# A two-block trunk on one core: the second block's bias table is written to memory one row per query and read back with a shifted step; constant products stand at the first block's norms

## The chip, the core and the metric

The kernel runs on one core of one Trainium2 chip. The metric is the device time of one execution in microseconds (us). TensorE (PE) multiplies, VectorE (DVE) and ScalarE (ACT) work element by element, GpSimd (POOL) does some element work and issues accumulating DMAs, and SyncE (SP) issues all other DMAs. All DMAs of the core run on the same 16 DMA engines.

## The reference

Two blocks run one after the other on x of 512 tokens by 1024 channels, each with two layers. Every layer has projections, attention and a feed-forward part with norms in between. What the change touches is the bias of the second block's windowed attention: `rel` is key minus query, a bucket function maps it to one of 32 buckets, and 16 heads have one value for each bucket.

```python
rel = jnp.arange(KEY_SPAN)[None, :] - WINDOW - jnp.arange(ATTN_BLOCK)[:, None]
band_bias = rel_bias.astype(f32)[t5_bucket(rel)].transpose(2, 0, 1)
...
s = jnp.einsum("bqgrd,bkgd->bgrqk", qb, kb,
               preferred_element_type=jnp.float32) * scale + bias
```

For one head this is a 128 x 384 tile (query by key) whose every row is the row above moved right by one. The first block's norms, at which the table is made, are

```python
x = x + rms_norm(mixed @ w_out, attn_post_gain)
h = rms_norm(x, ffn_pre_gain)
x = x + rms_norm(conv_ffn(h, ffn_w_up, ffn_conv_w, ffn_conv_b, ffn_w_down), ffn_post_gain)
```

## The kernel before

**Weights.** All weights stream through the core in chunks of eight 128 x 128 tiles (class `Stream`). A chunk is loaded into `raw` by SP (512 KB, line 301), ACT writes its negative to `lo` (line 311), POOL issues a DMA that reads the chunk from memory a second time and adds it to `lo` (line 312, 512 KB), and ACT or POOL rounds `raw` to `h` (line 316 or 314). So `h + lo` is the weight in two parts; the page calls them wh and wl. Each tile takes three products (lines 489 to 491), 24 for a chunk. There are four buffers of each kind. When the program reaches chunk c it emits the load of chunk c+6 and the conversion of chunk c+3; what it emits on SP, POOL and ACT then stands in their queues in that order.

**The norms.** `post_norm` (line 1329) ends the attention part and the feed-forward part of each of the first block's two layers: four norms. It sums squares on PE (`stat`), reduces them on DVE, takes the root on ACT and the reciprocal on DVE, spreads the result over all partitions on PE (`statb`), and then, for eight channel tiles m, DVE forms y (line 1341), DVE or POOL adds it to x (line 1342), ACT makes h of the tile before (line 403) and DVE its remainder hl (line 404). Then the residual is stored (xf or xa, eight DMAs of 256 KB) and the next group of products starts on h. `keep_warm(n)` multiplies a matrix of ones n times and nobody reads the result. I call the norms 1 to 4 in order of time; the chunk whose first product follows a norm is c.

**The table.** `bias_table` is a generator that is stepped by the caller (`side.step`). Its second step forms one row of 512 values for each head (`btab`, 16 partitions) and stores it as `tab_d`. Then it takes one head per step: SP reads 128 overlapping rows, each one element on from the last (`brev`), a product with the exchange matrix `exch` reverses their order (`bex`), ACT copies the result (`bout`) and SP stores it in `bias_d`. Two such steps come before norm 1, and every norm takes four more: one ahead of `rstd_a`, one behind it, two behind `spread`.

**Its readers.** In the second block `load_bias(h)` (line 1787) reads one head's 128 x 384 tile, two heads ahead of its use at line 1937, 16 times in each layer.

All engines run their instructions in the order in which the program emits them. The functions that the change touches:

Of the kernel before, what the change touches and what calls it, by code (L numbers as in the profile page):

```python
# [10 lines left out]
F32 = mybir.dt.float32  # L11
F32R = mybir.dt.float32r
I32 = mybir.dt.int32
AF = mybir.ActivationFunctionType
# [3 lines left out]
T = 512  # L18
# [6 lines left out]
NB, NO = 2, 2  # L25
XD = 30
GA, GB, GC = 1, 4, 1
NWU, NKW = 13, 6
NEG = -1.0e30
BIG = 3.0e38  # L30
TINY = 1e-30
# [121 lines left out]
def _consts():  # L153
    parts = []
    pos = 0

    def add(name, a):
        nonlocal pos
        a = np.asarray(a, np.float32)
        _CS[name] = (pos, a.shape[1])  # L160
        parts.append(a)
        pos += a.shape[1]

    p = np.arange(128)
    r, c = p[:, None], p[None, :]
    add("ident", np.eye(128))
    add("exch", np.eye(128)[::-1])
    add("maskA", np.concatenate([np.where(c > r, 0, NEG), np.where(c <= r, 0, NEG)], 1))
    add("maskC", np.concatenate([np.zeros((128, 384)), np.where(c <= r, 0, NEG)], 1))
    add("le", r <= c)  # L170
    add("ge", r >= c)
    add("gt", r > c)
    add("lt", r < c)
    n = np.arange(32)
    ok = np.stack([((n * 16 + 31)[None, :] <= (128 * i + p)[:, None]) & (n < 31)[None, :] for i in range(4)], 1)
    add("c01", ok.reshape(128, 128))
    add("cneg", np.where(ok, 0, NEG).reshape(128, 128))
    add("invf", (10000.0 ** (-(p % 32) / 32.0))[:, None])
    add("sign", np.where(p % 64 < 32, -1.0, 1.0)[:, None])
    return np.concatenate(parts, 1)  # L180


CONST = _consts()
NCST = CONST.shape[1]

# [61 lines left out]
def trunk_kernel(ctx: ExitStack, tc: tile.TileContext, xT, positions, wts, cst_d, oh_d, rb_d, cw1_d,  # L247
                 prm1_d, prm2_d, outT):
    nc = tc.nc
    layers = 2  # L250
    ctx.enter_context(tc.manual_schedule())
    V, A, G, PE = nc.vector, nc.scalar, nc.gpsimd, nc.tensor
# [4 lines left out]
    dpool = ctx.enter_context(tc.tile_pool(name="dpool", bufs=1, space=bass.MemoryType.DRAM))  # L257
# [4 lines left out]
    def big(name, dt=F32):  # L262
        return pools["t"].tile([128, T], dt, tag="t", name=name)

    def small(n, name, bufs=2):
        return pools["s"].tile([128, n], F32, tag=name, name=name, bufs=bufs)
# [4 lines left out]
    def bank(name, hold=False):  # L271
        b = banks.pop(0)
        t = psum.tile([128, T], F32, tag=f"b{b}", name=name)
        if hold:
            held[id(t)] = (b, t)
        else:
            banks.append(b)
        return t

    def free(t):  # L280
        banks.append(held.pop(id(t))[0])
# [105 lines left out]
    def C(name):  # L387
        o, n = _CS[name]
        return cst[:, o:o + n]
# [48 lines left out]
    def rstd_a(sq, n, act=False):  # L438

        sq.sums(len(sq.p))  # L440
        ps = sq.stat
        v = small(4, "var")
        V.tensor_reduce(v, ps[:, 0:128 * len(sq.p)].rearrange("p (a j) -> p j a", j=128)[:, 0:4, :], AX.X, OP.add)
        free(ps)
        r4 = small(4, "rs")
        if act:
            A.activation(v, v, AF.Sqrt, bias=epst, scale=1.0 / n)
            V.reciprocal(r4, v)
            return r4
        t4 = small(4, "rt")  # L450
        V.tensor_scalar(v, v, 1.0 / n, EPS, op0=OP.mult, op1=OP.add)
        V.tensor_scalar(r4.bitcast(I32), v.bitcast(I32), -0.5, float(0x5F3759DF), op0=OP.mult, op1=OP.add)
        for _ in range(3):
            V.tensor_mul(t4, r4, r4)
            V.scalar_tensor_tensor(t4, t4, -0.5, v, op0=OP.mult, op1=OP.mult)
            V.scalar_tensor_tensor(r4, t4, 1.5, r4, op0=OP.add, op1=OP.mult)
        return r4
# [5 lines left out]
    def keep_warm(n):  # L463

        t = bank("warm")
        for _ in range(n):
            PE.matmul(t[:, 0:128], ones, ones, start=True, stop=True)

    def spread(r4):

        pb = bank("statb", True)
        for j in range(4):
            PE.transpose(pb[:, 128 * j:128 * j + 128], r4[:, j:j + 1].to_broadcast([128, 128]), ident)
        return pb
# [79 lines left out]
    def prep(x, gcol, late=False):  # L554

        hs, sq = [], Squares(late=late)

        def f(m):
            h, lo = big("h", F32R), big("hl", F32R)
            split(h, lo, x[m], scale=gcol[:, m:m + 1])  # L560
            hs.append((h, lo))
        return hs, sq, f
# [221 lines left out]
    def layer1(l, x, hs, sq, gnext, side):  # L784
# [419 lines left out]
        for m in range(KT):  # L1204
# [7 lines left out]
            run(g)  # L1212
        ms.clear()
        hs, sq3 = post_norm(x, ys, pc("g2"), sq2, pc("g3"), side)


# [69 lines left out]
        ffn_order(pair, down)  # L1286
        x = xn
        hs, sq = post_norm(x, ys, pc("g4"), sq4, gnext(), side)
        if l:
            side.finish()  # L1290
# [38 lines left out]

    def post_norm(x, ys, gcol, sq, gnext, side):  # L1330

        side.step(1)
        r4 = rstd_a(sq, D, act=True)
        side.step(1)
        R = spread(r4)
        side.step(2)
        keep_warm(NKW)
        hs, sqn, f = prep(x, gnext)
        for m in range(KT):
            y = ys[m]  # L1340
            V.scalar_tensor_tensor(y, y, gcol[:, m:m + 1], R, op0=OP.mult, op1=OP.mult)
            (V if m % 2 == 0 else G).tensor_add(x[m], x[m], y)
            if m:
                f(m - 1)
        f(KT - 1)
        free(R)
        return hs, sqn


    bias_d = dpool.tile([128, 16, 384], F32, name="bias_d")  # L1350

    def bias_table():

        oh = big("oh")
        nc.sync.dma_start(oh[0:33, :], oh_d)
        rb = small(16, "rb", bufs=2)
        nc.sync.dma_start(rb[0:32, :], rb_d)
        V.memset(rb[32:33, :], NEG)
        yield
        ps = bank("btab")  # L1360
        PE.matmul(ps[0:16, :], rb[0:33, :], oh[0:33, :], start=True, stop=True)
        tb_ = big("btab")
        V.tensor_copy(tb_[0:16, :], ps[0:16, :])
        tab_d = dpool.tile([16, T], F32, name="tab_d")
        nc.sync.dma_start(tab_d, tb_[0:16, :])
        rev = {}
        for h in range(18):
            if h < 16:
                rev[h] = big("brev")
                nc.sync.dma_start(rev[h][:, 0:384], bass.AP(  # L1370
                    tensor=tab_d.tensor, offset=tab_d.offset + h * T, ap=[[1, 128], [1, 384]]))
            if h >= 2:
                pb = bank("bex")
                PE.matmul(pb[:, 0:384], C("exch"), rev.pop(h - 2)[:, 0:384], start=True, stop=True)
                o = big("bout")
                A.activation(o[:, 0:384], pb[:, 0:384], AF.Copy)
                nc.sync.dma_start(bias_d[:, h - 2, :], o[:, 0:384])
            yield

    masks = []  # L1380
# [7 lines left out]
    def layer2(l, x, hs, sq, gnext):  # L1388
# [396 lines left out]
        bias = {}  # L1785

        def load_bias(h):
            if h < 16:
                bias[h] = big("bias")
                nc.sync.dma_start(bias[h][:, 0:384], bias_d[:, h, :])  # L1790

        bias["load"] = load_bias
        load_bias(0)
        load_bias(1)
        pieces = [p for h in range(2, 16) for p in at(4 * h - 8, 2, head(h))]
        pieces += rest + at(7, 1, kx)
        pieces += [p for g in (2, 3) for p in at(17 + 8 * (g - 2), 2, pieces_of(stack_k(K, g, lambda: kT[1]), 4))]
        units = []
        for a in range(8):
            nm, den = small(8, "nm", bufs=8), small(8, "den", bufs=8)  # L1800
            o = {}
# [18 lines left out]
            for e in range(2):  # L1820
                h = 2 * a + e
# [96 lines left out]
        for m in range(KT):  # L1918
            o = big("out")
# [30 lines left out]
    with tc.tile_pool(name="spool1", bufs=2) as pools["s"]:  # L1950
        x = []
        hs, sq, f = prep(x, col(1, 0, P1, "g1")())
        keep_warm(NWU)
        for m in range(KT):
            load_x(x, m)
            if m % 2:
                W.load((m + 3) // 2)
            if m == 5:
                nc.sync.dma_start(cst, cst_d)
        for m in range(KT):  # L1960
            if m % 2 == 0:
                W.conv(m // 2 + 1)
            f(m)
        load_params(1, 1)
        side = Fill(bias_table())
        x, hs, sq = layer1(0, x, hs, sq, col(1, 1, P1, "g1"), side)
        load_params(2, 0)
        x, hs, sq = layer1(1, x, hs, sq, col(2, 0, P2, "n1"), side)
# [43 lines left out]
```

## Time and profile before

| | |
|---|---|
| time, median of 3 runs | 3266.52 us (3254.92 to 3266.82) |
| profiled execution: time, span | 3263.05 us, 3261.3 us |
| PE busy | 3097.5 us, 95% of the span |
| ACT, DVE, POOL busy | 1885.1, 1752.6, 759.9 us (58, 54, 23%) |
| mean granted TensorE clock | 0.979 of full |
| DMA moved | 547.30 MB, 168 GB/s on average |

A busy share says that an instruction was under way; matmuls are pipelined, so PE's 95% is not 95% of its peak. The span runs from the first to the last instruction; the time has 1.75 us more around it.

### The profile page before, as it was taken

The numbers are of one execution on the slowest core, as the hardware profiler recorded it, in microseconds if no ns is written. First come the engines' busy times: TensorE is split into PE (matmuls) and PEld (weight loads), VectorE is DVE, ScalarE is ACT, GpSimd is POOL, SyncE is SP. The second block draws the span as 40 slices with busy tenths as digits, with TensorE's granted clock in tenths as the row PEclk, the third lists the DMA queues.
The fourth block names the chain that finished last, engine by engine and source line by source line (L and its number), as shares of the span: only waits on it lengthen the run. The fifth ranks groups of instructions, "written<-read, shape, count | busy, mean of one in ns | idle before, by whom it ended". The sixth has DMA issues, their size and how long they took to land. (4 is left out here: it accounts for less than half of the span.)

```text
span 3261.3 us, 40685 instructions
## 1 busy us (share of the span) xinstructions
PE 3097.5 (95%) x14604; PEld 2543.5 (78%) x14604; DVE 1752.6 (54%) x3431; ACT 1885.1 (58%) x3288; POOL 759.9 (23%) x770
## 2 busy tenths in 40 slices
PE   8999999999899999999998889999999888999998
PEld 7878878887778877888786668788888666888887
DVE  5577355153477635424378987341326898734132
ACT  4578556464357756645476567554556656755453
POOL 2222211111222221111135422111112542211110
PEclk8999999999899999999999999999999989999999
DMA  9744769887964487989774334789897534488975
GB/s 273 169 104 91 196 177 206 195 202 188 231 145 106 91 210 186 204 188 224 182 172 110 96 93 111 196 201 219 199 224 167 116 77 114 99 202 202 224 183 140
DMA packets 170277, 547.30 MB, mean 168 GB/s; under 512 B 20011, under 2 KB 29227, under 8 KB 170076
## 3 DMA queue, kind: packets, MB, share of 16 engines
q0 software_dynamic: 66240, 241.20, 43.5%
q1 hardware_dynamic: 103836, 303.50, 26.7%
q8 instruction: 116, 1.90, 0.3%
q14 instruction: 85, 0.70, 0.1%
HBM read 516.81 MB, written 19.96 MB: 165 GB/s over the span
## 5 line engine op out<-in xcount | busy, mean ns | idle before, releaser
L490 PE MATMUL acc<-h,wl 128*128 128x512 f32 x2464 | 971.7, 394 | 36.3 <-DMA wl<-in_wts 36.2
L489 PE MATMUL acc<-h,wh 128*128 128x512 f32 x2464 | 994.7, 404 | 0.8 <-ACT h L403 0.8
L491 PE MATMUL acc<-hl,wh 128*128 128x512 f32 x2464 | 969.5, 393 | 0.2
L312 POOL DMA_DIRECT2D wl<-in_wts x460 | 398.6, 866 | 2030.0 <-ACT wl L311 1837.0
L311 ACT ACTIVATE wl<-wraw 128x1024 fp32r<-128x1024 f32 x460 | 482.9, 1050 | 299.2 <-PE acc L490 271.9
L490 PEld LDWEIGHTS acc<-h,wl 128*128 128x128 f32 x2464 | 469.3, 190 | 134.3 <-DMA wl<-in_wts 42.8
L491 PEld LDWEIGHTS acc<-hl,wh 128*128 128x128 f32 x2464 | 468.0, 190 | 100.7 <-DVE hl L404 1.5
L489 PEld LDWEIGHTS acc<-h,wh 128*128 128x128 f32 x2464 | 469.4, 190 | 95.7 <-issue 5.3
L316 ACT ACTIVATE wh<-wraw 128x1024 fp32r<-128x1024 f32 x400 | 417.3, 1043 | 0.0
L489 PE MATMUL acc<-ah,wh 128*128 128x512 f32 x704 | 274.4, 390 | 0.0
L491 PE MATMUL acc<-al,wh 128*128 128x512 f32 x704 | 274.1, 389 | 0.0
L490 PE MATMUL acc<-ah,wl 128*128 128x512 f32 x704 | 274.0, 389 | 0.0
L674 PE MATMUL pt<-cst,p 128*128 128x128 f32 x752 | 144.0, 279 | 24.3 <-ACT p L1939 9.5
L1229 ACT ACTIVATE c<-u,prm 128x512 f32<-128x512 f32 x88 | 71.1, 815 | 145.1 <-DVE u L1225 145.1
L489 PEld LDWEIGHTS acc<-ah,wh 128*128 128x128 f32 x704 | 132.2, 188 | 27.4
L491 PEld LDWEIGHTS acc<-al,wh 128*128 128x128 f32 x704 | 132.2, 188 | 27.4
L490 PEld LDWEIGHTS acc<-ah,wl 128*128 128x128 f32 x704 | 132.2, 188 | 27.2
L1225 DVE TENSOR_TENSOR u<-acc,R 128x512 f32<-128x512 f32 x88 | 60.0, 687 | 173.3 <-PE acc L491 173.2
L1085 ACT ACTIVATE p<-p,nm 128x128 f32<-128x128 f32 x192 | 102.1, 532 | 62.6 <-DVE nm L1083 60.6
L680 ACT ACTIVATE pth<-pt 128x256 fp32r<-128x256 f32 (+2 forms) x320 | 130.7, 411 | 9.6 <-PE pt L674 7.1
L674 PEld LDWEIGHTS pt<-cst,p 128*128 128x128 f32 x752 | 93.3, 141 | 51.5 <-ACT p L1939 17.9
L1895 DVE TENSOR_TENSOR x<-x,acc 128x512 f32<-128x512 f32 x32 | 22.0, 688 | 185.3 <-PE acc L491 171.7
(334 smaller groups left out, 5103.0 us busy)
## 6 DMA issues: line engine op xcount, KB each, us to landing
wraw<-in_wts SPq DMA_DIRECT2D x460, 512.0 KB, 6.7
wl<-in_wts POOLq DMA_DIRECT2D x460, 512.0 KB, 7.1
bias<-bias_d SPq DMA_DIRECT2D x32, 192.0 KB, 2.6
x<-in_xT SPq DMA_DIRECT2D x16, 256.0 KB, 8.4
cw<-in_cw SPq DMA_DIRECT2D x16, 256.0 KB, 6.3
xf<-x SPq DMA_DIRECT2D x16, 256.0 KB, 2.1
x<-xf SPq DMA_DIRECT2D x16, 256.0 KB, 10.1
xs<-x SPq DMA_DIRECT2D x16, 256.0 KB, 5.8
```

The lines of the kernel that those rows point to most:

```text
L311: A.activation(lo, r, AF.Copy, scale=-1.0)
L312: G.dma_start(out=lo, in_=wts[c], accum_op=OP.add)
L316: A.activation(h, r, AF.Copy)
L489: PE.matmul(acc, wh, xh, start=first, stop=False)
L490: PE.matmul(acc, wl, xh, start=False, stop=False)
L491: PE.matmul(acc, wh, xl, start=False, stop=last)
L674: PE.transpose(pt[:, 128 * n:128 * n + 128], t[:, 128 * (kb - b0):128 * (kb - b0) + 128], ident)
L680: A.activation(th[:, 0:w], pt[:, 0:w], AF.Copy)
L1085: A.activation(p[:, 0:w], p[:, 0:w], AF.Exp, bias=nm[:, col:col + 1], scale=-1.0, accum_out=den[:, col:col + 1])
L1225: V.tensor_mul(u, acc, st3["R"])
L1229: A.activation(c, u, AF.Identity, bias=cb[:, idx:idx + 1], scale=cw[:, 88 + idx:89 + idx])
L1895: V.tensor_add(x[m], x[m], acc)
```

## The change

`bias_table` keeps its row of 512 values per head but no longer stores `tab_d`, reads it back reversed, multiplies or copies. For each head one DMA reads the head's row, which lies in one partition of `btab`, 128 times and writes 128 rows of 512 values to `bias_d`, which is now 16 x 128 x 512 (256 KB a head). `load_bias` reads row q from element 127-q on, by a step of 511 between rows. `exch` leaves the constants. In `post_norm` all four steps come first, `keep_warm(3)` stands ahead of `spread`, and the products behind it are nine where they were six.

```diff
-NWU, NKW = 13, 6
+NWU, NKW = 13, 9
...
-    add("exch", np.eye(128)[::-1])
...
-        side.step(1)
+        side.step(4)
         r4 = rstd_a(sq, D, act=True)
-        side.step(1)
+        keep_warm(3)
         R = spread(r4)
-        side.step(2)
         keep_warm(NKW)
...
-    bias_d = dpool.tile([128, 16, 384], F32, name="bias_d")
+    bias_d = dpool.tile([16, 128, T], F32, name="bias_d")
...
-        tab_d = dpool.tile([16, T], F32, name="tab_d")
-        nc.sync.dma_start(tab_d, tb_[0:16, :])
-        rev = {}
-        for h in range(18):
-            if h < 16:
-                rev[h] = big("brev")
-                nc.sync.dma_start(rev[h][:, 0:384], bass.AP(
-                    tensor=tab_d.tensor, offset=tab_d.offset + h * T, ap=[[1, 128], [1, 384]]))
-            if h >= 2:
-                pb = bank("bex")
-                PE.matmul(pb[:, 0:384], C("exch"), rev.pop(h - 2)[:, 0:384], start=True, stop=True)
-                o = big("bout")
-                A.activation(o[:, 0:384], pb[:, 0:384], AF.Copy)
-                nc.sync.dma_start(bias_d[:, h - 2, :], o[:, 0:384])
+        for h in range(16):
+            nc.sync.dma_start(bias_d[h], tb_[h:h + 1, None, :].to_broadcast([1, 128, T]))
             yield
...
-                nc.sync.dma_start(bias[h][:, 0:384], bias_d[:, h, :])
+                nc.sync.dma_start(bias[h][:, 0:384], bass.AP(
+                    tensor=bias_d.tensor, offset=bias_d.offset + h * 128 * T + 127, ap=[[T - 1, 128], [1, 384]]))
```

On ACT at norm 1 stood, before, from the last squares of the norm to the next weights:

```order
L417 ACTIVATE sq<-acc 128x512
L1200 ACTIVATE y<-acc 128x512
L1376 ACTIVATE bout<-bex 128x384
L447 ACTIVATE var<-var,epst 128x4
L1376 ACTIVATE bout<-bex 128x384 x3
L403 ACTIVATE h<-x,prm 128x512 x8
L311 ACTIVATE wl<-wraw 128x1024
```

and now (the line numbers of the changed file are one lower there):

```order
L416 ACTIVATE sq<-acc 128x512
L1199 ACTIVATE y<-acc 128x512
L446 ACTIVATE var<-var,epst 128x4
L402 ACTIVATE h<-x,prm 128x512 x8
L310 ACTIVATE wl<-wraw 128x1024
```

The four copies are gone from between the root (`var`) and the first h. On PE at the same norm stood, before:

```order
L491 MATMUL acc<-ml,wh 128x512
L1374 MATMUL bex<-brev,cst 128x384
L434 MATMUL stat<-ones,sq 128x1 x4
L1374 MATMUL bex<-brev,cst 128x384
L473 MATMUL statb<-cst,rs 128x128 x4
L1374 MATMUL bex<-brev,cst 128x384 x2
L467 MATMUL warm<-ones 128x128 x6
L489 MATMUL acc<-h,wh 128x512
```

and now:

```order
L490 MATMUL acc<-ml,wh 128x512
L433 MATMUL stat<-ones,sq 128x1 x4
L466 MATMUL warm<-ones 128x128 x3
L472 MATMUL statb<-cst,rs 128x128 x4
L466 MATMUL warm<-ones 128x128 x9
L488 MATMUL acc<-h,wh 128x512
```

Products that waited for a DMA were exchanged for products that wait for nothing. SP's queue from the weights ahead of the table's row (`btab`) held, before, up to the second head's store:

```order
L301 DMA wraw<-in_wts 128x1024 x2
L1365 DMA tab_d<-btab 16x512
L1370 DMA brev<-tab_d 128x384
L301 DMA wraw<-in_wts 128x1024
L1370 DMA brev<-tab_d 128x384
L301 DMA wraw<-in_wts 128x1024 x4
L1370 DMA brev<-tab_d 128x384
L1377 DMA bias_d<-bout 128x384
L1370 DMA brev<-tab_d 128x384
L1377 DMA bias_d<-bout 128x384
```

and now up to the weights behind the stores:

```order
L300 DMA wraw<-in_wts 128x1024 x2
L1363 DMA bias_d<-btab 128x1x512
L300 DMA wraw<-in_wts 128x1024
L1363 DMA bias_d<-btab 128x1x512
L300 DMA wraw<-in_wts 128x1024 x4
L1363 DMA bias_d<-btab 128x1x512 x4
L372 DMA xf_4259<-x 128x512 x8
L300 DMA wraw<-in_wts 128x1024 x55
```

Two writes stand ahead of the last five weight loads before norm 1, four stand together ahead of the stores, and the weights of the feed-forward part come behind all of them. At norms 2 and 3 four writes stand so, at norm 4 two.

## Rows read from the trace of the kernel before

**Rows 1.** Page, costliest groups: busy us, mean ns, idle before and its releaser.

```profile
L490 PE MATMUL acc<-h,wl 128*128 128x512 f32 x2464 | 971.7, 394 | 36.3 <-DMA wl<-in_wts 36.2
```

**Rows 2.** Timeline of norm 1: start us, us, engine, line, operation, idle before.

```profile
414.04 0.65 PE L473 MATMUL statb<-cst,rs 128*128 128x128 f32 x4
415.50 0.69 DVE L1342 TENSOR_TENSOR x<-x,y 128x512 f32<-128x512 f32 x1
416.11 0.74 DVE L1341 SCALAR_TENSOR_TENSOR y<-y,prm,statb 128x512 f32<-128x512 f32 x1
416.83 0.91 PE L1374 MATMUL bex<-brev,cst 128*128 128x384 f32 x2 [1.50 <-DMA brev<-tab_d]
...
417.78 0.49 ACT L1376 ACTIVATE bout<-bex 128x384 f32<-128x384 f32 x1 [1.92 <-PE bex L1374]
418.17 1.32 ACT L403 ACTIVATE h<-x,prm 128x512 fp32r<-128x512 f32 x2
...
418.91 0.75 DVE L404 SCALAR_TENSOR_TENSOR hl<-x,prm,h 128x512 fp32r<-128x512 f32 x1 [2.06 <-ACT h L403]
```

**Rows 3.** Timelines of norms 2, 3 and 4: the first hl.

```profile
799.24 0.75 DVE L404 SCALAR_TENSOR_TENSOR hl<-x,prm,h 128x512 fp32r<-128x512 f32 x1 [1.88 <-ACT h L403]
...
1213.03 0.75 DVE L404 SCALAR_TENSOR_TENSOR hl<-x,prm,h 128x512 fp32r<-128x512 f32 x1 [2.25 <-ACT h L403]
...
1595.21 0.75 DVE L404 SCALAR_TENSOR_TENSOR hl<-x,prm,h 128x512 fp32r<-128x512 f32 x1 [2.50 <-ACT h L403]
```

**Rows 4.** Timelines behind norms 1, 2 and 3: weights that PE and ACT wait for.

```profile
432.88 1.04 ACT L311 ACTIVATE wl<-wraw 128x1024 fp32r<-128x1024 f32 x1
...
442.20 0.79 PE L490 MATMUL acc<-h,wl 128*128 128x512 f32 x1 [6.08 <-DMA wl<-in_wts]
...
822.09 0.80 PE L490 MATMUL acc<-h,wl 128*128 128x512 f32 x1 [5.65 <-DMA wl<-in_wts]
...
832.84 1.06 ACT L311 ACTIVATE wl<-wraw 128x1024 fp32r<-128x1024 f32 x1 [9.71 <-DMA wraw<-in_wts]
...
1235.97 0.79 PE L490 MATMUL acc<-h,wl 128*128 128x512 f32 x1 [5.74 <-DMA wl<-in_wts]
```

**Rows 5.** Busy time by stretch: length, PE busy (instructions), PEld, DVE, ACT, POOL, PEclk, DMA share, GB/s.

```profile
380.00:400.00 20.00, 20.00 (x87) 15.60 (x86) 2.67 (x4) 9.24 (x13) 2.59 (x3) 1.00 1.03 256
...
1236.00:1242.00 6.00, 6.00 (x15) 4.75 (x16) 0.71 (x2) 2.84 (x3) 1.72 (x2) 0.54 1.01 257
```

**Rows 6.** Page, DMA queues: packets, MB, share of 16 engines.

```profile
q0 software_dynamic: 66240, 241.20, 43.5%
q1 hardware_dynamic: 103836, 303.50, 26.7%
```

**Rows 7.** DMA issues: count, KB of one, median us from issue to landing.

```profile
bias<-bias_d SPq DMA_DIRECT2D x32, 192.0 KB, 2.6
...
xf<-x SPq DMA_DIRECT2D x16, 256.0 KB, 2.1
...
bias_d<-bout SPq DMA_DIRECT2D x16, 192.0 KB, 2.2
...
t<-kcb SPq DMA_DIRECT2D x4, 128.0 KB, 7.2
```

**Rows 8.** Timeline of SP's queue at the four norms: start us, us of issuing.

```profile
384.11 0.33 SPq L1365 DMA_DIRECT2D tab_d<-btab  x1
...
403.08 0.73 SPq L1370 DMA_DIRECT2D brev<-tab_d  x1
...
781.32 0.42 SPq L1370 DMA_DIRECT2D brev<-tab_d  x1
...
1197.01 0.42 SPq L1370 DMA_DIRECT2D brev<-tab_d  x1
...
1576.65 0.42 SPq L1370 DMA_DIRECT2D brev<-tab_d  x1
...
1612.37 16.09 SPq L301 DMA_DIRECT2D wraw<-in_wts  x6
```

## The prediction

> **What bounds the kernel now.** I read the page's costliest groups first. Nearly all of PE's time is the three-part weight products, and where PE sits idle for another engine in that group, it is for a weight chunk's second half: 36.2 us of 36.3 [rows 1]. So two things can move the time: the short chains in which PE has nothing to do, and the arrival of weights.
>
> Then the timeline of norm 1, since all removed instructions stand at the four norms. `statb` is done at 414.69, DVE has added the first tile of x by 416.19 and formed the second y by 416.85. Then DVE stands still for 2.06 us until ACT has made h. ACT could have begun h at about 416.2, but a `bout` copy stands ahead of it in its queue, that copy waits for the last `bex`, and that product waited for a `brev` read that SP had only just issued [rows 2]. At norms 2, 3 and 4 the same first hl waits 1.88, 2.25 and 2.50 us for the same reason [rows 3].
>
> Third, what follows a norm. PE runs through chunks c to c+2 and then stops at chunk c+3: 6.08 us at norm 1, 5.65 at norm 2, 5.74 at norm 3, each for wl [rows 4]. The conversion of that chunk stands on ACT behind the eighth h (432.88 at norm 1), and 9.3 us later PE can go on (442.20): the ACT copy, POOL's issue and the transfer. So the element chain of the norm sets when PE resumes, and a chain that is 2 us shorter is 2 us gained as long as transfers take what they take now.
>
> **The removed work.** The first h no longer waits. It could end some 0.05 us after the second y, so each norm gives nearly its wait: 2.0, 1.8, 2.2 and 2.4 us, together **-8.4 us**. The other parts of the reversing (16 copies, 16 products, 16 reads) lie in those waits or beside other work and give nothing more. The 3 + 9 constant products are cheap: six of them ahead of the first h are now nine, and PE has nothing else to do before h, nor would a late start of PE count, since it stops at c+3 anyway. So nothing for them.
>
> **The readers in the second block.** 32 reads of 192 KB land in 2.6 us at the median [rows 7], and each is issued two heads ahead. The new ones have as many rows and bytes, only another step. Even at three times the duration they are covered by a whole head of work: nothing.
>
> **The added writes.** Here is the unknown. 16 DMAs of 256 KB each draw all their bytes from one partition. The trace has no such DMA. From below: a store of 192 KB from 128 partitions lands in 2.2 us [rows 7], so about 2.5 us if the source doesn't matter. From above: SP's queue moved 303.5 MB in 26.7% of 16 engines' 3261.3 us [rows 6], which is 303.5e6 / (0.267 x 3261.3 x 16) = 21.8 GB/s for one engine and 349 GB/s for all. If one partition gives no more than one engine takes, a write takes 262,144 B / 21.8 GB/s = **12.0 us**, and all 16 engines stand in it. Which end is nearer? A copy from 64 partitions moves 128 KB in 7.2 us where a store from 128 partitions moves 256 KB in 2.1 us [rows 7]: half the source partitions, half the bytes, over three times as long. A part of that is waiting in the queue, but it leans strongly to the upper end, and one partition is far narrower than 64. I take 12.0 us.
>
> The Trainium skill has a rule that speaks against this change: its page "SBUF — State Buffer", section "Door 1: The DMA port swizzle", says that DMA bandwidth depends on how many of the 16 ports the partitions reach, and lists 27.6 GB/s measured for partitions 0 to 3. No run here shows that figure; by it a write would take about 9.5 us (estimate), and the sum below would come to about 3270.
>
> **What the writes hold up.** They go through SP's ring in order, ahead of the residual's stores and of the next weights. At 349 GB/s 256 KB take 0.75 us and 512 KB 1.5 us, and landing adds 1.6 us to the transfer (2.2 less 0.56 for 192 KB [rows 7]). The first load behind the stores is chunk c+6. After it has landed, 9.3 us pass until PE can use it, and PE asks for it three chunks after it resumed. A chunk of 24 products takes 5.5 us (87 products in 20.0 us [rows 5]), three take 16.6.
>
> - Norm 1: two writes go out at 384.1 and soon behind, five weight loads stand between and behind them (the order of SP's queue in the section on the change), four writes follow at 403.1 [rows 8]. 384.1 + 6 x 12.0 + 5 x 1.5 = 463.8; eight stores 6.0, the load 1.5 + 1.6: it lands at 472.9. Needed by 442.2 + 16.6 - 9.3 = 449.5 [rows 4]. **+23.4 us**.
> - Norm 3: four writes from 1197.0 [rows 8], over at 1245.1; stores and load: 1254.2. Needed by 1236.0 + 16.6 - 9.3 = 1243.3. **+10.9 us**.
> - Norm 2: four writes from 781.3, over at 829.4; eight stores and four loads of 256 KB 9.0, the load 3.1: 841.5. Before, ACT waited 9.71 us for this chunk until 832.84 [rows 4], and 9.3 us on from there lies behind the 838.7 at which PE, resumed at 822.1, is through three chunks, so this arrival already counts. **+8.7 us**.
> - Norm 4: only two writes are left, from 1576.7 to 1600.8, before the next load is issued at 1612.4 [rows 8]. Here the gain stays: **-2.4 us**.
>
> At norms 1 to 3 the gain of 2 us is swallowed, since PE then waits for chunk c+6 whatever the norm did. The sum is 23.4 + 10.9 + 8.7 - 2.4 = +40.6 us on the profiled execution's own time of 3263.05 us (0.1% under the median of the runs shown, 3266.52): **3304 us**.
>
> **The rivals.**
>
> 1. *Slower, as above*, 3304: its own range is 3285 to 3332. The upper end comes from POOL's accumulating transfers, which share the engines with the writes: one takes 43.5% x 3261.3 / 460 = 3.1 us of all engines [rows 6] (460 chunks), and three more of them ahead of the late load at each of three norms make 28 us. Chance 0.58.
> 2. *Worse than that*: the accumulating transfers themselves crawl beside the writes, so that chunk c+3 is late too and ACT, blocked on a late chunk before norm 1, delays the norm. Above 3332. Chance 0.07.
> 3. *The weights' lead covers the writes.* The lateness vanishes at norm 2 if a write takes under 9.8 us (12.0 - 8.7/4), at norm 3 under 9.3 and at norm 1 under 8.1. At 9 us only norm 1 is late, by 5: 3266, with 3255 to 3272 as its range. For it: four buffers of each kind, and the estimate from the page above. Against it: I counted no time for the transfers of rival 1's upper end. Chance 0.18.
> 4. *Not slower: the source doesn't matter.* A write lands in 2.5 us, all of the 8.4 us is gained: 3254.6. It decides as soon as a write takes well under 8 us. For it: the four writes together then move fewer bytes than reads and stores do now (1.0 against 1.5 MB). Against it: the copy from 64 partitions. Chance 0.13.
> 5. *Faster by more*: rival 4, and the pauses at c+3 become short enough for PE to keep its clock. Behind norm 3 the granted clock was 0.54 and 15 products took 6.0 us [rows 5] where they take 3.45 at full clock, 2.55 lost; three times that and 8.4 make 16 us: 3247. Against it: PE and the weights move together, so that the pause keeps its length. Chance 0.04.
>
> **How the numbers follow.** About 0.5%, 16 us, is what a measurement of this kernel can tell from no change. Rivals 1 and 2 are slower by more than that (0.65), 3 and 4 within it (0.31), 5 faster (0.04). The predicted time is rival 1's. The range reaches down to rival 4 and up to the upper end of rival 1: 3253 to 3332 leaves out 2 and 5, about 0.11.
>
> **What the profile after would show.** Of the gain: the first hl waits 0.1 us for h where it waited about 2, and no other instruction stands between `var` and h on ACT. Of the loss: the `bias_d` writes land 12 us apart or more, the first weight load behind norm 1 lands near 473, ACT's wl copies wait for `wraw` by 10 to 20 us behind norms 1 to 3, and PE's idle time for wl rises from 36 us to some 75. At norm 4 no wait is longer than now. I am wrong if a write lands in under 8 us, or if weights stand ready though it takes 12, which would mean that the rings don't hold each other up as I assume.

## The result: slower by 0.9%

The changed kernel takes 3292.15 us (median of 4 runs, 3287.83 to 3294.57), the kernel before 3265.69 us in the same comparison: a ratio of 1.0088 with a 95% interval of 1.0069 to 1.0107. The profiled execution of the changed kernel takes 3292.98 us (span 3291.2 us), 29.9 us more than that of before, and the two traces are compared with each other.

The page's costliest group, which answers to [rows 1], holds nearly all of it: PE's idle time for a weight chunk's second half went from 36.2 to 64.9 us.

```profile
L489 PE MATMUL acc<-h,wl 128*128 128x512 f32 x2464 | 972.4, 395 | 65.0 <-DMA wl<-in_wts 64.9
```

**Where PE waits.** The timelines behind norms 1 to 4 of the changed kernel, first PE's waits for wl, then ACT's for raw weights, answer to [rows 4]:

```profile
413.69 0.79 PE L489 MATMUL acc<-mh,wl 128*128 128x512 f32 x1 [4.91 <-DMA wl<-in_wts]
450.80 0.80 PE L489 MATMUL acc<-h,wl 128*128 128x512 f32 x1 [10.91 <-DMA wl<-in_wts]
839.52 0.80 PE L489 MATMUL acc<-h,wl 128*128 128x512 f32 x1 [15.82 <-DMA wl<-in_wts]
865.05 0.50 PE L489 MATMUL acc<-h,wl 128*128 128x512 f32 x1 [0.20 <-DMA wl<-in_wts]
1261.53 0.80 PE L489 MATMUL acc<-h,wl 128*128 128x512 f32 x1 [17.66 <-DMA wl<-in_wts]
1646.83 0.79 PE L489 MATMUL acc<-h,wl 128*128 128x512 f32 x1 [5.71 <-DMA wl<-in_wts]
...
465.49 1.06 ACT L310 ACTIVATE wl<-wraw 128x1024 fp32r<-128x1024 f32 x1 [13.53 <-DMA wraw<-in_wts]
856.55 1.06 ACT L310 ACTIVATE wl<-wraw 128x1024 fp32r<-128x1024 f32 x1 [20.74 <-DMA wraw<-in_wts]
1275.60 1.06 ACT L310 ACTIVATE wl<-wraw 128x1024 fp32r<-128x1024 f32 x1 [19.62 <-DMA wraw<-in_wts]
```

There is one long wait behind each of norms 1 to 3, longer than before by 4.8, 10.2 and 11.9 us, and a new one of 4.9 us ahead of norm 1; norm 4 is nearly as it was (5.7 us, 4.9 before). The three longer waits and the new one come to 31.8 us. ACT does wait 13 to 21 us for raw weights, as forecast, but PE hardly notices: where chunk c+6 is then needed it waits 0.20 us behind norm 2, and none of its waits behind the long ones is over 1.1 us.

**Which transfer is late.** PE resumes at 450.80 and at 839.52. The transfers that land at these times are the last that POOL issued *before* the norm's first h, those of chunk c+2; SP had issued the norm's four writes 4 to 7 us earlier. Time of issue (behind the comma) and from issue to landing, norms 1 and 2:

```profile
L311 POOL DMA_DIRECT2D wl<-in_wts x1: 865/865/865, 417.4 to 417.4; - x1
DMA to landing us min/median/max: 33.4/33.4/33.4
...
L311 POOL DMA_DIRECT2D wl<-in_wts x1: 862/862/862, 799.5 to 799.5; - x1
DMA to landing us min/median/max: 40.0/40.0/40.0
```

417.4 + 33.4 = 450.8, and 799.5 + 40.0 = 839.5. At norm 3 it is 1222.2 + 39.2 = 1261.4. In the kernel before, the same transfer took 7.2, 7.3 and 5.6 us, chunk c+2 was there in time, and PE stopped one chunk later. At norm 1 of the kernel before:

```profile
L312 POOL DMA_DIRECT2D wl<-in_wts x1: 862/862/862, 407.5 to 407.5; - x1
DMA to landing us min/median/max: 7.2/7.2/7.2
```

At norm 4, with two writes, it took 22.7 us and PE did not wait for it.

**What the writes do meanwhile.** Two stretches behind norm 3 (columns as in [rows 5]):

```profile
1230.00:1234.00 4.00, 2.62 (x15) 1.81 (x14) 3.77 (x5) 1.44 (x2) 1.27 (x1) 1.00 0.90 27
1234.00:1237.00 3.00, 3.00 (x15) 2.48 (x14) 2.97 (x6) 0.72 (x1) 1.35 (x1) 1.00 0.98 29
```

The DMA engines are busy for 90 to 98% of the time and move 27 to 29 GB/s together, less than a tenth of the 349 GB/s that SP's queue moves on average for its busy time. At that rate a write of 256 KB takes 9.0 to 9.7 us. The trace's records of single packets say more: a packet of 2,048 bytes of such a write takes 1.09 us, and POOL's queue moves no data at all from 1222.3 to 1239.0, though chunk c+2's transfer was issued at 1222.2. At all four norms that transfer lands 3 to 4 us behind the last of the slow packets.

**Where the gain stands.** Norm 1 of the changed kernel, which answers to [rows 2]:

```profile
424.12 0.65 PE L472 MATMUL statb<-cst,rs 128*128 128x128 f32 x4
...
426.31 0.72 ACT L402 ACTIVATE h<-x,prm 128x512 fp32r<-128x512 f32 x1 [2.46 <-DVE x L1340]
427.02 1.27 POOL L1340 TENSOR_TENSOR x<-x,y 128x512 f32<-128x512 f32 x1 [8.77 <-DVE y L1339]
427.07 1.78 DVE L403 SCALAR_TENSOR_TENSOR hl<-x,prm,h 128x512 fp32r<-128x512 f32 x1
```

The first h comes 2.19 us behind `statb` instead of 4.13, and the first hl has no wait left. But this hl takes 1.78 us where it took 0.75: POOL's addition runs beside it now. Before, that addition lay in the 2 us in which DVE stood still.

### The profile page after: what moved, and what is told of

Read it like the earlier page. It is cut to its first block, busy times and chain, and to the rows that moved or that the text cites. A ratio compares the mean times of both kernels' runs of the same rounds, so it can differ in the third digit from the quotient of the medians.

```text
span 3291.2 us, 40668 instructions
## 1 busy us (share of the span) xinstructions
PE 3094.0 (94%) x14620; PEld 2544.3 (77%) x14620; DVE 1760.6 (53%) x3431; ACT 1878.0 (57%) x3272; POOL 759.2 (23%) x770
## 5 line engine op out<-in xcount | busy, mean ns | idle before, releaser
L489 PE MATMUL acc<-h,wl 128*128 128x512 f32 x2464 | 972.4, 395 | 65.0 <-DMA wl<-in_wts 64.9
L310 ACT ACTIVATE wl<-wraw 128x1024 fp32r<-128x1024 f32 x460 | 482.8, 1050 | 335.1 <-PE acc L489 252.1
```

The costliest lines, as they stand in the source:

```text
L310: A.activation(lo, r, AF.Copy, scale=-1.0)
L489: PE.matmul(acc, wl, xh, start=False, stop=False)
```

## Experiments

Ratios are to the kernel before, measured on the same chip (median 3259 to 3261 us there), with 95% intervals. This table gives, for the kernels that matter for it, how long the last transfer issued before each norm took to land:

| kernel | writes at norms 1 to 4 | us to landing at norms 1, 2, 3, 4 |
|---|---|---|
| before | none from one partition | 7.2, 7.3, 5.6, 7.7 |
| changed | 4, 4, 4, 2 (and 2 ahead of norm 1) | 33.4, 40.0, 39.2, 22.7 |
| writes from memory | the same | 8.2, 8.3, 7.5, 5.6 |
| two writes a norm | 2, 2, 2, 2 | 22.5, 22.0, 22.0, 22.0 |
| partitions h and h+64 | 4, 4, 4, 2 (and 2) | 8.0, 9.8, 11.0, 8.2 |
| partitions h and h+32 | 4, 4, 4, 2 (and 2) | 13.9, 13.4, 14.7, 14.8 |

**The source alone.** Row and places as in the change, only read from memory:

```diff
+        tab_d = dpool.tile([16, T], F32, name="tab_d")
+        nc.sync.dma_start(tab_d, tb_[0:16, :])
         for h in range(16):
-            nc.sync.dma_start(bias_d[h], tb_[h:h + 1, None, :].to_broadcast([1, 128, T]))
+            nc.sync.dma_start(bias_d[h], bass.AP(
+                tensor=tab_d.tensor, offset=tab_d.offset + h * T, ap=[[0, 128], [1, T]]))
```

> The row of 512 values per head is stored once (32 KB), and each of the 16 writes reads its row 128 times from memory instead of from one partition; number, size, place and order of the writes stay. Theory A (one partition gives only about 27 GB/s, so that each write holds all 16 engines for some 9 us, and the accumulating transfers that share the engines land late): writes land in 2 to 5 us, PE waits for wl behind norms 1 to 3 by 5 to 6 us as before, time 3255 to 3262. Theory B (the writes hold SP's ring in order and the weight loads behind them come late, by reason of their 256 KB and their place, not of their source): 3285 to 3295, as the changed kernel. Theory C (moved steps and added constant products cost the time): 3285 to 3295 too.

Measured: 3256.72 us, ratio 0.9989 (0.9979 to 0.9998). PE's idle time for wl is 36.3 us, that of the kernel before. The writes land in 7.5 us at the median, more than expected, which costs nothing here. Behind norm 3 the engines are busy for 35% and move 131 GB/s where the change had 90% and 27 GB/s:

```profile
1203.00:1207.00 4.00, 2.61 (x15) 1.81 (x14) 3.77 (x5) 1.44 (x2) 1.27 (x1) 1.00 0.35 131
...
439.86 0.80 PE L489 MATMUL acc<-h,wl 128*128 128x512 f32 x1 [5.79 <-DMA wl<-in_wts]
```

Theories B and C fall as causes of the loss: moved steps, constant products, and writes of this number, size and place are all still there. The source makes the loss.

**The order alone, twice.** First the changed kernel with the norm's steps where they had been:

```diff
-        side.step(4)
+        side.step(1)
         r4 = rstd_a(sq, D, act=True)
-        keep_warm(3)
+        side.step(1)
         R = spread(r4)
+        side.step(2)
...
-NWU, NKW = 13, 9
+NWU, NKW = 13, 6
```

> The changed kernel with the norm's steps where they were (one ahead of the root, one behind it, two behind the spread) and six constant products, none ahead of the spread. On SP the writes stand where they stand now, up to an issue time of a microsecond. Theory A and B: 3287 to 3297, as the changed kernel. Theory C: 3255 to 3268.

Measured: 3289.93 us, 1.0096 (1.0079 to 1.0113), as the changed kernel. Then the kernel before with the new order and the new products, the same edit in reverse:

> The kernel before with only the norm's part of the change: four steps of the old table ahead of the root, three constant products ahead of the spread, nine behind it. Theory A and B (the writes are the loss): no loss of that kind; the four copies now stand ahead of the root on ACT and hold it until the reads have landed, 2 to 4 us a norm in place of the 2 us behind it, so 3262 to 3278. Theory C (the moved steps and constant products are the loss): 3285 or more.

Measured: 3285.22 us, 1.0078 (1.0063 to 1.0093). A miss, and by its number the case of theory C. The rows of norm 1 (PE, then ACT) show another cause: the products of the reversing now stand ahead of the sums on PE, and the fourth waits for its read, which SP issues only behind a store.

```profile
418.05 1.62 PE L1373 MATMUL bex<-brev,cst 128*128 128x384 f32 x2 [3.74 <-DMA brev<-tab_d]
419.46 1.70 PE L434 MATMUL stat<-ones,sq 128*128 128x1 f32 x8
...
419.70 0.49 ACT L1375 ACTIVATE bout<-bex 128x384 f32<-128x384 f32 x1 [4.87 <-PE bex L1373]
421.40 0.30 ACT L447 ACTIVATE var<-var,epst 128x4 f32<-128x4 f32 x1 [1.21 <-DVE var L443]
```

The root waits behind this at every norm: between the last transfer that POOL issues ahead of a norm and the first behind it lie 5.4 to 7.0 us more than in the kernel before. So the four steps and the old table cost time together; with a table that needs no product (the kernel from memory) they cost nothing.

**Another ring.** `nc.sync` becomes `nc.scalar` in the line of the writes.

> The 16 writes are issued by ACT instead of SP, so that they lie in a ring of their own and no weight load or store stands behind them in order. The source stays one partition. Theory A1 (the loss is on the accumulating transfers, whose packets take turns with the slow ones on each engine): chunk c+3 is still late, PE waits 11 to 18 us for it behind norms 1 to 3, and the time stays at 3280 to 3300. Theory B (the loss is in SP's order): ACT's waits for wraw of 13 to 21 us behind norms 1 to 3 vanish, and the time falls to 3255 to 3265.

Measured: 3317.74 us, 1.0178 (1.0163 to 1.0193), outside both cases. ACT's rows at norm 1 (ACTq is its issuing):

```profile
422.31 17.02 ACTq L1363 DMA_DIRECT2D bias_d<-btab  x3
439.38 0.30 ACT L446 ACTIVATE var<-var,epst 128x4 f32<-128x4 f32 x1 [16.51 <-issue]
```

ACT stood 17 us in issuing three writes, and the root behind them was late by as much. At the norms this tells nothing of A1 against B, since the whole norm was put off; it does show that ACT, issuing such writes, is held up itself. Ahead of norm 1, though, two writes go out on ACT's ring at 383.0 and 389.6, and POOL's transfers issued at 385.1, 391.9 and 397.4 land in 21.8, 18.7 and 17.1 us, where those of the kernel before took some 6 to 9. So the writes hold up POOL's transfers without standing in SP's ring.

**How many are free.** Eight heads' rows only, two writes a norm and none ahead of norm 1:

```diff
-        side.step(4)
+        side.step(2)
...
-        for h in range(16):
+        for h in range(0, 16, 2):
```

> Again 8 heads' rows (the others take their neighbour's bias), now two at each of the four norms and none ahead of norm 1. Two writes take about 19 us and are over when POOL issues the transfer of chunk c+3, some 19 us behind the norm's start; four take 38 and are not. Theory A with this threshold: no loss at any norm, 3253 to 3261, PE's wait at c+3 5 to 6 us at all four. Theory D: 3268 to 3275, PE's waits longer at each norm by some 4 us.

Measured: 3256.10 us, 0.9988 (0.9978 to 0.9997): free. It was a close thing. The transfer of chunk c+2 takes 22.5 us at norm 1 and lands at 434.0; PE asks for it at 433.8, and the pause at c+3 is as ever:

```profile
434.06 0.50 PE L489 MATMUL acc<-h,wl 128*128 128x512 f32 x1 [0.26 <-DMA wl<-in_wts]
444.69 0.79 PE L489 MATMUL acc<-h,wl 128*128 128x512 f32 x1 [4.91 <-DMA wl<-in_wts]
```

So the place of the threshold was expected rightly and its reason not: it is c+2, issued before the writes are over, and not c+3.

**Elsewhere.** The same eight writes, one at a time, in the second layer's attention:

```diff
-        side.step(4)
...
+        if l:
+            pieces += at(3, 7, [lambda: side.step(1)] * 8)
         run_units(units, LAG, f_br,
```

> Only 8 of the 16 heads' rows are written (the others take their neighbour's bias, which changes the result of the second block), none at a norm: one write at a time, some 10 to 20 us apart, in the second layer's attention of the first block, where the DMA share is 0.34 to 0.47 of the engines. Each still reads one partition. Theory A (a write costs time only where POOL's transfers need the engines within the lead that the program has): 3253 to 3260, PE's waits for wl behind the norms 5 to 6 us as before. Theory D (every write costs its own 9 us or a fixed part of it wherever it stands, about 33 us for 16 and so 16 for 8): 3268 to 3275.

Measured: 3258.13 us, 0.9992 (0.9983 to 1.0002). The writes fill engines that had been idle (the stretch from 1050 to 1080 has a DMA share of 0.82, that of the kernel before 0.44), and PE is busy throughout this stretch:

```profile
1050.00:1080.00 30.00, 30.00 (x181) 26.26 (x181) 22.84 (x66) 23.83 (x62) 6.41 (x6) 1.00 0.82 122
```

Theory D falls: a write has no price of its own where the engines have room for it.

**One partition or what it shares.** The table's rows stand twice in SBUF, and a write takes 64 rows from each copy:

```diff
-            nc.sync.dma_start(bias_d[h], tb_[h:h + 1, None, :].to_broadcast([1, 128, T]))
+            nc.sync.dma_start(bias_d[h].rearrange("(a q) t -> a q t", a=2),
+                              tb_[h:h + 65:64, None, :].to_broadcast([2, 64, T]))
```

> All 16 writes, at their places; the table's rows stand twice in SBUF, in partitions h and h+64, and each write takes 64 rows from either. If two partitions give twice what one gives, a write takes 4.7 us, four are over in 19 us, and the loss at norms 1 to 3 goes as at norm 4: 3254 to 3264, GB/s of the write's stretch about 55 instead of 27. If a repeated row is slow in itself: 3286 to 3296. The Trainium skill's page SBUF — State Buffer, section Door 1: The DMA port swizzle, has h and h+64 on different ports.

> As the kernel with partitions h and h+64, but with h and h+32. If the limit belongs to the single partition, this is as fast as that one: 3254 to 3264. If it belongs to something that the two partitions share, nothing changes against the changed kernel: 3286 to 3296, 27 GB/s. The Trainium skill's page SBUF — State Buffer, section Door 1: The DMA port swizzle, has h and h+32 on one port, by which the second would be seen.

Measured: 3261.99 us, 1.0010 (1.0000 to 1.0020), with h and h+64; 3322.59 us, 1.0199 (1.0184 to 1.0214), with h and h+32 (33 and 32 in the place of 65 and 64). A stretch of norm 1 with little but writes under way, first of h and h+64, then of h and h+32:

```profile
424.00:427.00 3.00, 3.00 (x15) 2.46 (x14) 2.97 (x6) 0.72 (x1) 1.44 (x1) 1.00 0.13 51
```

```profile
436.00:439.00 3.00, 3.00 (x15) 2.49 (x14) 2.76 (x5) 1.32 (x2) 0.77 (x1) 1.00 0.12 25
```

In this form the engines are busy for 0.12 to 0.13 in both kernels, as if two of 16 did the work (2/16 is 0.125). Two engines' worth on h and h+64 moves 51 GB/s, as much on h and h+32 moves 25, and 16 engines on h alone moved 27. So the limit is neither the engine nor the single partition; h and h+32 share it. The Trainium skill's page "SBUF — State Buffer", section "Door 1: The DMA port swizzle", has this sharing and 27.6 GB/s for partitions 0 to 3; the trace agrees with both. The kernel with h and h+64 is not quite free: PE waits 9.4 and 8.3 us at c+3 behind norms 1 and 3, its idle time for wl is 43.6 us in all, and its interval lies above that of the writes from memory.

That h and h+32 came out 30 us slower than the change was not expected. Chunk c+2 is in time there, landing in 13.4 to 14.8 us. Chunk c+3 is late, and then chunk c+6 as well, because its raw weights are (behind norm 2 ACT converts it at 877.6, after a wait of 30.4 us, and its transfer lands at 886.1): the `xf` stores ahead of them in SP's ring land in 26.1 us at the median, and ACT waits 110.5 us for raw weights in all, where the changed kernel's ACT waits 82.9. Behind norm 2, PE at c+3 and at c+6:

```profile
860.97 0.79 PE L489 MATMUL acc<-h,wl 128*128 128x512 f32 x1 [20.43 <-DMA wl<-in_wts]
886.15 0.80 PE L489 MATMUL acc<-h,wl 128*128 128x512 f32 x1 [5.25 <-DMA wl<-in_wts]
```

The second wait is the mechanism of my prediction; it is 3.7, 5.3 and 5.7 us behind norms 1 to 3.

**The pause at c+3.** The writes from memory, and one line more behind `keep_warm(NKW)`; then the same line in the changed kernel:

```diff
         keep_warm(NKW)
+        W.conv(W.conved + 1)
         hs, sqn, f = prep(x, gnext)
```

> The kernel whose writes read memory, and behind the spread of each norm the conversion of chunk c+3 is put ahead of the eight h on ACT, where ACT stood idle for 2.46 us; POOL issues that chunk's transfer some 15 us earlier. If the pause at c+3 has its cause in the ACT copy's place behind the eighth h, it goes at all four norms; chunk c+4, still converted behind the eighth h, is then the next to be late, by 1 to 2 us. So 4 us a norm or more, 16 us in all: 3238 to 3246 where the kernel before has 3260. If the transfer is late for another reason (the weights themselves are not there): no change, 3256.

Measured: 3236.96 us, 0.9927 (0.9914 to 0.9939), the fastest of all. The conversion stands in ACT's idle time ahead of the first h, and PE's idle time for wl falls from 36.3 to 22.4 us, 13.9 of the 20 us that this kernel gains on the one without the new line; the rest was not followed up. The conversions and the first h of norm 1, and pauses that are left at norms 2 and 4:

```profile
415.67 1.04 ACT L310 ACTIVATE wl<-wraw 128x1024 fp32r<-128x1024 f32 x1
416.62 1.04 ACT L315 ACTIVATE wh<-wraw 128x1024 fp32r<-128x1024 f32 x1
418.23 0.72 ACT L402 ACTIVATE h<-x,prm 128x512 fp32r<-128x512 f32 x1 [0.57 <-DVE x L1341]
...
817.56 0.50 PE L489 MATMUL acc<-h,wl 128*128 128x512 f32 x1 [1.99 <-DMA wl<-in_wts]
1599.22 0.80 PE L489 MATMUL acc<-h,wl 128*128 128x512 f32 x1 [3.61 <-DMA wl<-in_wts]
```

> The changed kernel, its writes from one partition as they are, with the same early conversion. Chunk c+3 is then there in time. Theory A alone (only the accumulating transfer of c+3 is held up, and nothing else is late): the loss goes with the pause, 3240 to 3260. Theory A with B behind it (SP's ring is over at the same time whatever PE does, so that chunk c+6 comes when it came, and PE now waits there what it waited at c+3): 3280 to 3292, PE's long waits at norms 1 to 3 of 10 us and more at chunks c+4 to c+6, ACT's waits for wraw 13 to 21 us.

Measured: 3285.97 us, 1.0081 (1.0066 to 1.0097). The number is that of "A with B behind it", but the expectation took c+3 for the late chunk, and it is c+2. Its transfer, issued at 418.2, lands 35.4 us later, and PE waits for it as in the changed kernel; the early one of c+3 only joins it behind the same writes:

```profile
L311 POOL DMA_DIRECT2D wl<-in_wts x1: 862/862/862, 425.7 to 425.7; - x1
DMA to landing us min/median/max: 30.5/30.5/30.5
...
453.61 0.79 PE L489 MATMUL acc<-h,wl 128*128 128x512 f32 x1 [13.09 <-DMA wl<-in_wts]
```

**The half of the gain that stayed away.** The writes from memory, with `(V if m % 2 == 0 or m == 1 else G)` for the addition:

> The kernel whose writes read memory, with the second tile's addition on DVE instead of POOL. The first hl took 1.77 us there and 0.75 in the kernel before; if that is POOL's addition running beside it, it takes 0.75 again, and DVE's own addition costs 0.69: the eighth h comes 0.3 to 1 us earlier behind the root, and the time falls by 1 to 4 us, which this measurement can hardly tell from none (3252 to 3257). If the hl is longer for another reason, it stays at 1.77 and the eighth h comes 0.7 later.

Measured: 3252.17 us, 0.9978 (0.9969 to 0.9987). The first hl with POOL's addition beside it (writes from memory), and without (this kernel):

```profile
415.80 1.27 POOL L1340 TENSOR_TENSOR x<-x,y 128x512 f32<-128x512 f32 x1 [8.61 <-DVE y L1339]
415.85 1.77 DVE L403 SCALAR_TENSOR_TENSOR hl<-x,prm,h 128x512 fp32r<-128x512 f32 x1
```

```profile
413.83 0.69 DVE L1340 TENSOR_TENSOR x<-x,y 128x512 f32<-128x512 f32 x1
414.44 0.74 DVE L403 SCALAR_TENSOR_TENSOR hl<-x,prm,h 128x512 fp32r<-128x512 f32 x1
```

The Trainium skill's page "SBUF — State Buffer", section "Who interferes with whom", says that DVE and GpSimd share one port pair by an exclusive lock; 1.77 against 0.74 us agrees. From `statb` to the first conversion behind the eighth h it is now 17.4 us at norm 1, and 1.7 us are won back at the four norms together, so this explains a part of the gain that stayed away and not all of it. All three edits together:

> Writes from memory, early conversion of chunk c+3 and the second tile's addition on DVE together. The early conversion gave 20 us over the writes from memory alone and the addition 4.5; both shorten what stands before a chunk converted behind the eighth h, so they should add up nearly, less what chunk c+4 now sets: 3231 to 3237 where the kernel before has 3260. If c+4's arrival no longer depends on the eighth h, the addition gives nothing more: 3236 to 3239.

Measured: 3239.75 us, 0.9939 (0.9925 to 0.9953). It is not faster than without the addition on DVE: the intervals overlap, and the idle time for wl is 23.1 us here and 22.4 there. The two gains do not add up.

## Why the prediction was right, and where it was not

Direction and range hold: 3304 forecast, in 3253 to 3332, and 3292.15 measured; on the profiled executions +40.6 us forecast and +29.9 measured. But the two steps that make the number are both off, and their errors partly cancel: that 3304 came as near as it did is in part luck, since the mechanism that I forecast, with the write rightly sized, gives 5 us and not 30.

- **A write takes 12.0 us: mis-sized.** It takes 9.0 to 9.7. I put one partition equal to one engine's average of 21.8 GB/s; the limit is 25 to 29 GB/s, and h+32 shares it while h+64 does not. The lean to the upper end was right, and the estimate of 9.5 us from the Trainium skill's page was nearer than mine.
- **"What the writes hold up": wrong.** I let SP's ring set the end: writes, then stores, then the load of chunk c+6, which PE would wait for. That load was late (ACT waited 13 to 21 us), but no PE wait that followed from it is over 1.1 us. With 9.5 us in the place of 12.0 my sum would have been 23.4 less 6 x 2.5 at norm 1, 10.9 less 4 x 2.5 at norm 3, and the gains of 1.8 and 2.4 at norms 2 and 4: +5.1 us, where 29.9 were measured. (My "about 3270" for that case left out norm 2's gain, and rival 3's 3266 those of norms 2 and 3; with them it is 3268 and 3262.) What PE waited for was in the other queue: the accumulating transfer of chunk c+2, issued by POOL before the norm, which took 33 to 40 us instead of 7 beside four writes. Rival 2 named this mechanism, with c+3 and at a price above 3332; it is the mechanism that acted, at a smaller price.
- **Norm 1 also lost 4.9 us ahead of it**, behind the two writes at 385.7 and 386.9. In the sum I had these only as a delay of what comes after; rival 2 had a late chunk before norm 1, though as a wait of ACT.
- **Norm 4 keeps its time: right.** Two writes are covered. I had no lateness there because the next load is issued later; the runs show that two writes, 22 us, are just about what chunk c+2 has in hand.
- **-8.4 us of gain: half of it.** From `statb` to the first conversion behind the eighth h it is 412.89 to 430.83, 17.94 us, in the kernel from memory, where before it is 414.04 to 432.88 [rows 2, 4], 18.84. So 0.9 us is gained at norm 1, not 2.0; at the others 1.0, 1.1 and 1.6, 4.6 in all. The interval of that kernel's ratio, 0.7 to 6.8 us faster, holds 4.6 and not 8.4. The removed wait had covered POOL's addition, which then ran into the first hl; moving that addition to DVE won back 1.7 of the 3.8 us that were missing, and where the rest went was not traced.
- **The readers and the constant products: nothing**, as said. Reads of `bias_d` land in 2.5 us (2.6 before), and the kernel from memory holds both edits without a loss.
- **Signs.** PE's idle time for wl was to be some 75 us and is 64.9, and the first raw weights behind norm 1 were to land near 473 and are there at 465.5. The condition "or if weights stand ready though it takes 12" did not arise in either form: raw weights were late, and PE was not stopped by them.

What stays open: why a transfer in another queue gets through only when nearly all the writes are over; no run separated this. Nor was it tried in the changed kernel whether the late raw weights would cost PE time if chunk c+2 came early. The kernel with h and h+32, in which it does, says that they can.

## What to carry to other kernels

A DMA that repeats one SBUF row kept all 16 engines busy here at some 27 GB/s, so its price was paid by whatever else needed the engines; put the row in memory first and repeat it from there, or place the writes where the engines idle. When a burst of transfers is put in, look first at those that other queues have already under way, not only at what stands behind it in its own. And before a wait is counted as gain, see what other engines do in it.

## What the hardware showed that was not expected

- Two copies of the source 32 partitions apart give no more than one (25 against 27 GB/s), 64 apart give twice as much (51).
- A DMA written as two times 64 rows kept the engines busy for 0.12 to 0.13, two of 16, where the one with 128 rows from one partition kept 0.90 and more of them busy.
- A transfer of 512 KB that lands in 7 us takes 22 us beside two such writes and 33 to 40 beside four, though it is in another queue; behind norm 3 that queue moved no data for 16.7 us.
- ACT, issuing three such writes, stood for 17 us.
